# Neighbourhood queries and keys written with channels on partitions, and the recurrent branch woven in by its 48 steps

## The chip, the cores and the metric

One core of one Trainium2 chip runs the whole program. The metric is the device time in microseconds (us) of one execution, lower being better. Engines: PE (TensorE) multiplies, ACT (ScalarE), DVE (VectorE) and POOL (GpSimd) work elementwise, SP only issues DMAs; ACT issues DMAs too.

## The reference

Two layers of a block over 1280 tokens (256 of context, 1024 latent) of width 1024, in fp32. Each layer projects the modulated input `x` and feeds four branches: A, neighbourhood attention; B, latent attention; C, a gated linear recurrence; D, grouped-query attention. What matters here is the projection of A and the recurrence C:

```python
lat = split_cols(p_lat[..., :MIX_COLS], MIX_SPLITS)      # p_lat = modulated x @ w_in
q, k, v = (split_heads(tt, NA_HEADS) for tt in lat[0:3]) # branch A: 256 + 256 + 256 columns
...
x_c = centred_depthwise_conv(x, conv_w, conv_b)          # branch C
r = sigmoid(x_c @ w_a + b_a); i = sigmoid(x_c @ w_x + b_x)
log_a = -LRU_C * r * softplus(-lam)
a = exp(log_a); u = sqrt(-expm1(2.0 * log_a)) * (i * x_c)
h = linear_scan(a, u, h0, reverse)                       # one scan per direction, summed
```

The second layer has no use for queries of the context tokens.

## The kernel before, in words

**Precision.** Each fp32 operand is held as a high and a low half, and a product is three passes on PE: high by high, high by low, low by high. So a projection of 128 tokens over 1024 input channels is 8 chunks of 128 channels times 3 passes, 24 products. `x` lies in SBUF with channels on partitions, so that either operand can stand still: `mm_a` (L294, products at L299 to L301) holds 128 tokens of `x` in the array and streams weights, giving tokens on partitions; `mm_b` (L303, L307 to L309) holds 128 columns of weights and streams tokens, giving channels on partitions.

**Branch A's projection**, `a_steps` (L801), uses `mm_a`: per tile of 128 tokens it streams 512 columns (256 of queries, 256 of keys) into one PSUM bank; the second layer's two context tiles stream the 256 columns of keys alone. ACT copies the queries' half, scaled by 1/8 (L808), and the keys' half (L809) to SBUF. One tile later `put_t` (L340) turns it: four PE transposes (L348) into another bank, an ACT cast to the high half (L312), a DVE subtraction for the low half (L313), and two DMAs on ACT's queue (L355) to `qk_a` in DRAM, in runs of 128 tokens. Ten more tiles of 256 columns give the values (`put_v`, L358: cast, subtraction, one DMA at L362). `project` (L388) does eight tiles one by one and the last two chunk by chunk together.

**Branch C**, `lru_steps` (L470), goes twice over 128 channels (c = 0, 1). Each time: 24 products per token group into the three-bank tile `wide` (`sbank`), ACT copies (L481), DVE's convolution (L484, L489), a cast and a subtraction (L312, L313), then for each direction six sets of three gate products into `wide` with sigmoids on ACT (L515), and the chain tanh (L522) and exp (L523) on ACT, L526, L527 and L521 on DVE, square root on ACT (L528), L529 and two scans (L531, L532 or L535, L537) on DVE. ACT loads a table of functions (ACT_TABLE_LOAD) when it changes between sigmoid or tanh, exp, and square root. Then the directions are added (L541), and the branch's SiLU gate z is projected by `put_u` (L440; L459, L460, L466), and the result stored (L468).

**What sets the order.** `weave` (L83) runs streams of steps, always the one with the smallest (done + 0.5) / n; n is a number that the caller gives. Here (L950) the main stream, `m_proj`, one step of loads for the first attention, then `a_proj`, has n = W_A = 30, and the recurrence n = W_B = 26. The main stream has 33 steps in each layer (12 + 1 + 20); the recurrence has 48 in the first and 40 in the second. A scheduler behind that orders each engine's instructions by their dependences, so the printed orders below are not the programmed order to the step. The attention loop starts when both streams have ended; `cut_memory` (L953) closes the pool of large tiles and opens a new one over the same memory, so the first score tile of attention (written by L641) takes memory that the recurrence has used. `g_att__mm` are products of the merge gates, which fill PE between the score products (L639), transposes (L584) and value products (L591, L592) of attention.

**Buffers.** `mm` is a ring of two PSUM banks, shared by the projections, z and the gates; the high halves `ph` have three SBUF buffers, the low halves `pl` two.

Of the kernel before, what the change touches and what calls it, by code (L numbers as in the profile page):

```python
# [8 lines left out]
F32 = mybir.dt.float32  # L9
F32R = mybir.dt.float32r  # L10
AF = mybir.ActivationFunctionType
ALU = mybir.AluOpType
# [5 lines left out]
KC = D // 128  # L18
# [15 lines left out]
G_LAG = 1  # L34
X_ACT = (0, 2)
M_ORDER = (2, 3, 1, 0)
W_A = 30
W_B = 26
Z_0, GATE_0 = 2, 10
UNITS = [(2, 3), (5, 3), (8, 2)]  # L40
AHEAD = 2
# [6 lines left out]
def hybrid_kernel(ctx: ExitStack, tc, a):  # L48
    nc = tc.nc
    pe, act, dve, pool, sp = nc.tensor, nc.scalar, nc.vector, nc.gpsimd, nc.sync  # L50
# [3 lines left out]
    tp = ctx.enter_context(tc.tile_pool(name="tp", bufs=2))  # L54
# [21 lines left out]
    def nm(s):  # L76
        ids[0] += 1
        return f"{phase[0]}__{s}_{ids[0]}"
# [32 lines left out]
    def mm():  # L111
        return ps_mm.tile([128, 512], F32, tag="mm", name=nm("mm"))
# [9 lines left out]
    def tbank():  # L122
        turns[2] = (turns[2] + 1) % 3
        if wide_t[0] and not turns[2]:
            return ps_v.tile([128, 512], F32, tag="pv", name=nm("t"))
        return ps_t.tile([128, 512], F32, tag="t", name=nm("t"))
# [20 lines left out]
    def tmp(w=512, dt=F32):  # L147
        return tp.tile([128, w], dt, tag="tmp", name=nm("tmp"), bufs=3)
# [154 lines left out]
    def mm_b(ps, ws, xs, first=True, last=True):  # L303
        nk = len(ws)
        for k in range(nk):
            (wh, wl), (xh, xl) = ws[k], xs(k)
            pe.matmul(ps, wh, xh, start=first and k == 0, stop=False)  # L307
            pe.matmul(ps, wh, xl, start=False, stop=False)  # L308
            pe.matmul(ps, wl, xh, start=False, stop=last and k == nk - 1)  # L309

    def hi_lo(hi, lo, src):
        act.copy(hi, src)  # L312
        dve.tensor_sub(lo, src, hi)  # L313

    def layer(l, xh, xl, need_ctx, gate, finish, side, ahead=None):
        w_in = a["w_in"][l]
        q0t = 0 if need_ctx else CT
        groups = [(0, 256), (256, 512), (768, 512)]
        qgroups = groups if need_ctx else groups[1:]
# [7 lines left out]
        def xs_g(g):  # L327
            gs = slice(g[0], g[0] + g[1])
            return lambda k: (xh[:, k, gs], xl[:, k, gs])

        def dram(shape, dt, s):
            return dr.tile(shape, dt, tag=s, name=nm(s))

        qk_a = dram([2, 4, 128, NT], F32, "qka")
# [8 lines left out]
        def put_t(dst, t, first, src):  # L343

            n = len(src)
            pt = tbank()
            for i, s in enumerate(src):
                pe.transpose(pt[:, i * 128:(i + 1) * 128], s, ident)  # L348
            hi = tp.tile([128, 4, 128], F32R, tag="ph", name=nm("th"), bufs=3)
            lo = tp.tile([128, 4, 128], F32R, tag="pl", name=nm("tl"), bufs=2)  # L350
            p3 = pt.rearrange("p (a b) -> p a b", a=4)
            hi_lo(hi[:, :n, :], lo[:, :n, :], p3[:, :n, :])
            ts = slice(t * 128, (t + 1) * 128)
            for d, s in enumerate((hi, lo)):
                act.dma_start(dst[d, first:first + n, :, ts].rearrange("c p t -> p c t"), s.bitcast(F32)[:, :n, :])  # L355
# [20 lines left out]
        def project(ws, first_col, n, take=mm):  # L376

            for t in range(TT - 2):
                ps = take()
                c0 = first_col(t)  # L380
                mm_a(ps[:, c0:n], xs_t(t), ws, c0, n)
                yield t, ps
            c0 = first_col(TT - 2)
            last = [(t, mm()) for t in range(TT - 2, TT)]
            for k in range(KC):
                for t, ps in last:
                    xs = xs_t(t)
                    mm_a(ps[:, c0:n], lambda j: xs(k), ws[k:k + 1], c0, n, k == 0, k == KC - 1)  # L388
            yield from last
# [410 lines left out]

        def a_steps():  # L801
            wa = load_rows(w_in, C_A, 512)
            prev = None
            for t, ps in project(wa, lambda t: 0 if t >= q0t else 256, 512):
                c0 = 0 if t >= q0t else 256
                y = tmp()
                if c0 == 0:
                    act.activation(y[:, :256], ps[:, :256], AF.Copy, scale=0.125)  # L808
                act.copy(y[:, 256:], ps[:, 256:])  # L809
                if prev:  # L810
                    put_t(*prev)
                prev = qk_a, t, c0 // 128, [y[:, c:c + 128] for c in range(c0, 512, 128)]
                yield
            put_t(*prev)
            wv = load_rows(w_in, C_AV, 256)
            for t, ps in project(wv, lambda t: 0, 256):
                put_v(v_a, t, ps[:, :256].rearrange("p (h e) -> p h e", e=64))
                yield
# [126 lines left out]
        def first_loads():  # L945
            next(att)
            yield


        weave(("", chain((f"m_proj{l}", m_steps()), (f"g_att{l}", first_loads()), (f"a_proj{l}", a_steps())), W_A),  # L950
              (f"lru{l}", lru_steps(), W_B))
        wide_t[0] = False
# [93 lines left out]
        for batch in batches:  # L1046
            pairs = [(t, slot(w=D, s="Y")) for t in batch]
            for h in range(2):
# [5 lines left out]
                for t, Y in pairs:  # L1054
                    if chunks:
                        split_sum(chunks.pop(0))
                    s = 1 if t < CT else 0
# [3 lines left out]
                    ps = bank()  # L1061
# [205 lines left out]
```

## Time and profile before

| | us |
|---|---|
| median of three runs (2957.03 to 2962.0) | 2960.34 |
| the profiled execution's own time | 2960.92 |
| its span in the trace | 2959.1 |
| PE busy in the span | 2790.4 (94%) |
| DVE, ACT, POOL busy | 1508.0, 1219.0, 418.8 |

Times in the trace are counted from the start of the span; 1.8 us of the execution lie outside it. In the trace the first layer's `a_proj` runs on PE from 217 to 374 us and its recurrence from 125 to 404 us, and attention begins at 399 us; in the second layer `a_proj` runs from 1821 to 1968 us, the recurrence from 1726 to 1984 us, and attention begins at 1985 us. Rows of a stretch give busy time of each engine, and PEclk, the granted clock of TensorE as a share of its full speed. The bracket behind an instruction is the idle time of its engine before it and what ended that. A matmul's duration includes the time to drain; what the stream pays is the distance from one start to the next.

### The profile page before, as it was taken

The page shows a single profiled execution, that of the slowest core. Times are in us where ns is not written, and L with a number is a line of the kernel's source. Part 1 is how long each engine was busy: PE and PEld are TensorE (multiplying, and loading weights), DVE is VectorE, ACT ScalarE, POOL GpSimd, SP SyncE. Part 2 cuts the span into 40 slices and gives each one's busy share as a digit, 9 for nine tenths or more (in the row PEclk, how much of TensorE's full clock was granted, in tenths as well). Part 3 has the DMA queues.
Part 4 walks back from the last instruction along what each step waited for, and adds up shares of the span by engine and source line. Part 5 has one row for each costly group of instructions (what it writes and reads, how often), then busy time and mean ns, then how long its engine had stood idle before and what let it go on. Part 6 is the DMA issues. An engine that isn't in the chain of part 4 may idle for free.

```text
span 2959.1 us, 40218 instructions
## 1 busy us (share of the span) xinstructions
PE 2790.4 (94%) x14458; PEld 2253.0 (76%) x14458; DVE 1508.0 (51%) x3069; ACT 1219.0 (41%) x2631; POOL 418.8 (14%) x507
## 2 busy tenths in 40 slices
PE   7997979999999999899999798999999999999998
PEld 3785858888888887677767576778888888777776
DVE  5644266555555552232458554356555556533456
ACT  4344256445455542222234434346545455522230
POOL 1210020110111100111222120012111111001131
PEclk9998989999999999999999898999999999999999
DMA  6333322222223333333332333423222323222232
GB/s 248 115 107 102 107 72 84 84 84 87 88 88 123 103 98 111 104 120 104 124 98 90 91 103 111 117 74 102 80 93 78 106 103 126 87 94 87 86 109 91
DMA packets 240424, 301.83 MB, mean 102 GB/s; under 512 B 27488, under 2 KB 160096, under 8 KB 240224
## 3 DMA queue, kind: packets, MB, share of 16 engines
q1 hardware_dynamic: 134368, 225.58, 24.2%
q10 hardware_dynamic: 105856, 73.68, 8.0%
q8 instruction: 114, 1.87, 0.3%
q14 instruction: 86, 0.70, 0.1%
HBM read 217.11 MB, written 82.07 MB: 101 GB/s over the span
## 4 chain that ended last, share of the span: by engine, by line
PE 75%; DVE 7%; DMA 4%; ACT 4%; issue 2%; POOL 2%; ACTq 1%; SPq 0%; DVEq 0%; POOLq 0%
PE wide L639 6%; PE merge__mm L307 4%; PE merge__mm L308 4%; PE merge__mm L309 4%; PE wide L307 3%; PE wide L308 3%; PE wide L309 3%; PE m_att__t L584 3%; PE g_att__t L584 2%; PE a_att__mm L307 2%; PE a_att__mm L308 2%; PE a_att__mm L309 2%; PE m_att__mm L309 2%; PE m_att__mm L308 2%; PE m_att__mm L307 2%
## 5 line engine op out<-in xcount | busy, mean ns | idle before, releaser
L307 PE MATMUL merge__mm<-xh,merge__whi 128*128 128x512 f32 (+1 forms) x640 | 243.0, 380 | 0.9 <-ACT a_att__tmp L934 0.9
L308 PE MATMUL merge__mm<-xl,merge__whi 128*128 128x512 f32 (+1 forms) x640 | 239.6, 374 | 0.0
L309 PE MATMUL merge__mm<-xh,merge__wlo 128*128 128x512 f32 (+1 forms) x640 | 239.4, 374 | 0.0
L313 DVE TENSOR_TENSOR m_att__pl<-m_att__t,m_att__ph 128x384 fp32r<-128x384 f32 (+1 forms) x248 | 122.1, 508 | 117.2 <-ACT m_att__ph L312 78.8
L263 ACT CAST merge__whi<-merge__wraw 128x256 fp32r<-128x256 f32 (+1 forms) x128 | 65.6, 513 | 255.6 <-PE merge__mm L308 176.7
L1002 DVE TENSOR_TENSOR merge__tmp<-wide,merge__tmp 128x512 f32<-128x512 f32 (+1 forms) x120 | 76.5, 637 | 184.8 <-PE wide L309 161.2
L1003 POOL TENSOR_TENSOR merge__acc<-merge__acc,merge__tmp 128x512 f32<-128x512 f32 (+1 forms) x60 | 79.2, 1320 | 585.9 <-DVE merge__tmp L1002 585.8
L307 PEld LDWEIGHTS merge__mm<-xh,merge__whi 128*128 128x128 f32 x640 | 120.6, 188 | 44.5 <-issue 19.9
L312 ACT CAST m_att__ph<-m_att__t 128x384 fp32r<-128x384 f32 (+1 forms) x248 | 105.0, 439 | 115.3 <-PE m_att__t L584 103.5
L313 DVE TENSOR_TENSOR g_att__pl<-g_att__t,g_att__ph 128x384 fp32r<-128x384 f32 (+1 forms) x228 | 111.3, 514 | 79.6 <-ACT g_att__ph L312 58.4
L307 PE MATMUL wide<-merge__uh,merge__whi 128*128 128x256 f32 (+1 forms) x320 | 127.4, 398 | 20.4 <-ACT merge__uh L312 11.5
L264 DVE TENSOR_TENSOR merge__wlo<-merge__wraw,merge__whi 128x256 fp32r<-128x256 f32 (+1 forms) x128 | 71.0, 555 | 141.2 <-ACT merge__whi L263 134.3
L309 PEld LDWEIGHTS merge__mm<-xh,merge__wlo 128*128 128x128 f32 x640 | 120.8, 189 | 23.9 <-issue 0.4
L308 PEld LDWEIGHTS merge__mm<-xl,merge__whi 128*128 128x128 f32 x640 | 120.8, 189 | 22.3
L312 ACT CAST g_att__ph<-g_att__t 128x384 fp32r<-128x384 f32 (+1 forms) x228 | 97.7, 446 | 69.3 <-PE g_att__t L584 65.3
L307 PE MATMUL a_att__mm<-xh,a_att__whi 128*128 128x512 f32 (+1 forms) x320 | 123.8, 387 | 0.0
L641 DVE TENSOR_SCALAR_CACHE_REDUCE m_att__p<-wide 128x1280 f32<-128x1280 f32 (+1 forms) x72 | 98.7, 1371 | 42.1 <-PE wide L639 41.8
L309 PE MATMUL a_att__mm<-xh,a_att__wlo 128*128 128x512 f32 (+1 forms) x320 | 120.1, 377 | 0.0
L639 PE MATMUL wide<-g_att__ks,g_att__q 128*128 128x512 f32 (+1 forms) x400 | 103.5, 365 | 17.5 <-DVE g_att__p L641 16.3
L308 PE MATMUL a_att__mm<-xl,a_att__whi 128*128 128x512 f32 (+1 forms) x320 | 120.0, 375 | 0.0
L299 PE MATMUL a_proj__mm<-a_proj__whi,xh 128*128 128x256 f32 (+1 forms) x320 | 112.0, 351 | 8.1 <-ACT a_proj__tmp L809 4.5
L308 PE MATMUL wide<-merge__ul,merge__whi 128*128 128x256 f32 (+1 forms) x320 | 119.6, 374 | 0.0
(418 smaller groups left out, 7919.4 us busy)
## 6 DMA issues: line engine op xcount, KB each, us to landing
merge__wraw<-in_w_chunks_dram SPq DMA_DIRECT2D x64, 256.0 KB, 2.9
mod__wm<-in_w_mod_dram SPq DMA_DIRECT2D x64, 256.0 KB, 3.0
g_proj__wm<-in_w_mod_dram SPq DMA_DIRECT2D x16, 512.0 KB, 9.8
a_att__wraw<-in_w_chunks_dram SPq DMA_DIRECT2D x32, 256.0 KB, 2.7
merge__wraw<-in_w_branch_dram SPq DMA_DIRECT2D x64, 128.0 KB, 2.1
merge__tmp<-start__gates SPq DMA_DIRECT2D x32, 256.0 KB, 3.2
merge__tmp<-outp__gates SPq DMA_DIRECT2D x32, 256.0 KB, 3.4
g_att__wraw<-in_w_chunks_dram SPq DMA_DIRECT2D x28, 256.0 KB, 2.7
```

Source lines behind the costliest of these rows:

```text
L264: (pool if by_pool else dve).tensor_sub(lo[:, :n], raw[:, :n], hi[:, :n])
L299: pe.matmul(ps, xh, wh[:, n0:n1], start=first and k == 0, stop=False)
L307: pe.matmul(ps, wh, xh, start=first and k == 0, stop=False)
L308: pe.matmul(ps, wh, xl, start=False, stop=False)
L309: pe.matmul(ps, wl, xh, start=False, stop=last and k == nk - 1)
L312: act.copy(hi, src)
L313: dve.tensor_sub(lo, src, hi)
L584: pe.transpose(tb[:, i * 128:(i + 1) * 128], pts[q0 + i][:, col:col + 128], ident)
L639: pe.matmul(wide[:, c0:c0 + w], qs[:, j, qi * 128:(qi + 1) * 128], k[:, c0:c0 + w], start=j == 0, stop=j == len(ks) - 1)
L641: dve.tensor_scalar(pt[:, :nk], wide[:, :nk], -scale, None, ALU.mult, ALU.min, accum_out=nb)
L1002: dve.tensor_mul(sgm[:, :g[1]], pb[:, :g[1]], sgm[:, :g[1]])
L1003: (pool if w is None else dve).tensor_add(acc[c][:, gs], acc[c][:, gs], sgm[:, :g[1]])
```

## The change

Queries and keys are projected by `mm_b`: for each of the four blocks of 128 columns and each token group (256, 512 and 512 tokens; the second layer's queries leave out the first) the weights stand still and the tokens stream. The bank then holds channels on partitions already, so the transposes and the tile between are gone: one ACT operation writes the high half, scaled for queries (L814), one DVE operation the low half (L815), and two DMAs on ACT's queue store them (L817) in runs of 256 or 512 tokens. Twelve such items take the place of ten tiles in the first layer, ten items in the second. The values' part is as it was. W_A becomes 32 and W_B 48. The main stream then has 35 steps in the first layer and 33 in the second.

```diff
-W_A = 30
-W_B = 26
+W_A = 32
+W_B = 48
...
         def a_steps():
             wa = load_rows(w_in, C_A, 512)
-            prev = None
-            for t, ps in project(wa, lambda t: 0 if t >= q0t else 256, 512):
-                c0 = 0 if t >= q0t else 256
-                y = tmp()
-                if c0 == 0:
-                    act.activation(y[:, :256], ps[:, :256], AF.Copy, scale=0.125)
-                act.copy(y[:, 256:], ps[:, 256:])
-                if prev:
-                    put_t(*prev)
-                prev = qk_a, t, c0 // 128, [y[:, c:c + 128] for c in range(c0, 512, 128)]
+            items = [(c, g) for c in range(4) for g in (qgroups if c < 2 else groups)]
+
+            def part(c, g, ps, ks):
+                xs = xs_g(g)
+                ws = [(wh[:, c * 128:(c + 1) * 128], wl[:, c * 128:(c + 1) * 128]) for wh, wl in wa]
+                mm_b(ps[:, :g[1]], [ws[k] for k in ks], lambda j: xs(ks[j]), ks[0] == 0, ks[-1] == KC - 1)
+
+            def keep(c, g, ps):
+                n, scale = g[1], 0.125 if c < 2 else 1.0
+                hi = tp.tile([128, 512], F32R, tag="ph", name=nm("th"), bufs=3)
+                lo = tp.tile([128, 512], F32R, tag="pl", name=nm("tl"), bufs=2)
+                act.activation(hi[:, :n], ps[:, :n], AF.Copy, scale=scale)
+                dve.scalar_tensor_tensor(lo[:, :n], ps[:, :n], scale, hi[:, :n], ALU.mult, ALU.subtract)
+                for d, s in enumerate((hi, lo)):
+                    act.dma_start(qk_a[d, c, :, g[0]:g[0] + n], s.bitcast(F32)[:, :n])
+
+            for c, g in items[:-2]:
+                ps = mm()
+                part(c, g, ps, list(range(KC)))
+                keep(c, g, ps)
                 yield
-            put_t(*prev)
+
+            last = [(c, g, mm()) for c, g in items[-2:]]
+            for k in range(KC):
+                for c, g, ps in last:
+                    part(c, g, ps, [k])
+            for c, g, ps in last:
+                keep(c, g, ps)
+                yield
             wv = load_rows(w_in, C_AV, 256)
             for t, ps in project(wv, lambda t: 0, 256):
                 put_v(v_a, t, ps[:, :256].rearrange("p (h e) -> p h e", e=64))
```

**Where the instructions stand: the end of the first layer's projections, PE.** The four `wide` products with `lru__` operands are gate products of the second channel block (c = 1), `g_att__mm` products of the merge gates, and L639 attention's scores. Before, from the last gate products on:

```order
L309 MATMUL wide<-lru__lruh_3281,lru__gl_3296 128x256
L307 MATMUL g_att__mm_3524<-xh,g_att__whi_3514 128x256
L308 MATMUL g_att__mm_3524<-xl,g_att__whi_3514 128x256
L307 MATMUL g_att__mm_3652<-xh,g_att__whi_3514 128x512
L307 MATMUL wide<-lru__lruh_3281,lru__gh_3295 128x512
L308 MATMUL wide<-lru__lrul_3282,lru__gh_3295 128x512
L309 MATMUL wide<-lru__lruh_3281,lru__gl_3296 128x512
```

With the change, the last products ahead of attention's scores at the same place:

```order
L301 MATMUL a_proj__mm_3398<-a_proj__whi_3093,xl 128x256
L299 MATMUL a_proj__mm_3399<-a_proj__whi_3093,xh 128x256
L300 MATMUL a_proj__mm_3399<-a_proj__wlo_3094,xh 128x256
L301 MATMUL a_proj__mm_3399<-a_proj__whi_3093,xl 128x256
L639 MATMUL wide<-g_att__ks_2376,g_att__q_2380 128x256 x2
L584 MATMUL g_att__t_3514<-ident,g_att__p_3469 128x128
```

The gate products of c = 1 no longer stand there; the last pair of value tiles (`a_proj__mm_3398` and `3399`) does.

**The same place, DVE.** L526 to L541 and L466 are the recurrence's last chain, L641 is attention's first evacuation of scores. Before:

```order
L526 TENSOR_TENSOR lru__lruo_3366<-lru__lrug_3336 128x1280
L527 SCALAR_TENSOR_TENSOR lru__lrut_3362<-lru__lruo_3366,lru__lrut_3362 128x1280
L521 TENSOR_TENSOR lru__lrug_3349<-lru__lrug_3349,lru__lruc_3273 128x1280
L529 TENSOR_TENSOR lru__lrug_3349<-lru__lrug_3349,lru__lrut_3362 128x1280
L535 SCALAR_TENSOR_TENSOR lru__lruo_3366<-lru__lrug_3336,lru__lrug_3349 128x256
L537 SCALAR_TENSOR_TENSOR lru__lruo_3366<-lru__lrug_3336,lru__lruo_3366,lru__lrug_3349 128x1024
L541 TENSOR_TENSOR lru__lruo_3329<-lru__lruo_3329,lru__lruo_3366 128x1280
L466 SCALAR_TENSOR_TENSOR lru__lruo_3329<-lru__lruo_3329,lru__tmp_3411 128x256
L466 SCALAR_TENSOR_TENSOR lru__lruo_3329<-lru__lruo_3329,lru__tmp_3440 128x512
L466 SCALAR_TENSOR_TENSOR lru__lruo_3329<-lru__lruo_3329,lru__tmp_3469 128x512
L641 TENSOR_SCALAR g_att__p_3487,g_att__nb_3488<-wide 128x256
```

With the change:

```order
L466 SCALAR_TENSOR_TENSOR lru__lruo_2849<-lru__lruo_2849,lru__tmp_3335 128x512
L313 TENSOR_TENSOR a_proj__vt_3364<-a_proj__mm_3339,a_proj__vt_3364 128x4x64
L313 TENSOR_TENSOR a_proj__vt_3394<-a_proj__mm_3369,a_proj__vt_3394 128x4x64
L641 TENSOR_SCALAR g_att__p_3469,g_att__nb_3470<-wide 128x256
L313 TENSOR_TENSOR a_proj__vt_3448<-a_proj__mm_3398,a_proj__vt_3448 128x4x64
L313 TENSOR_TENSOR a_proj__vt_3452<-a_proj__mm_3399,a_proj__vt_3452 128x4x64
L641 TENSOR_SCALAR g_att__p_3475,g_att__nb_3476<-wide 128x256
```

The scans and sums have gone from in front of L641; four evacuations of value tiles stand around it.

**Where the chain has gone: DVE in the query and key part, with the change.** L815 frees the PSUM bank of an item (`a_proj__mm`), L526 to L532 are the first direction's chain of c = 1:

```order
L815 SCALAR_TENSOR_TENSOR a_proj__tl_2840<-a_proj__mm_2814,a_proj__th_2839 128x512
L526 TENSOR_TENSOR lru__lruo_2849<-lru__lrug_2788 128x1280
L527 SCALAR_TENSOR_TENSOR lru__lrut_2845<-lru__lruo_2849,lru__lrut_2845 128x1280
L521 TENSOR_TENSOR lru__lrug_2801<-lru__lrug_2801,lru__lruc_2704 128x1280
L529 TENSOR_TENSOR lru__lrug_2801<-lru__lrug_2801,lru__lrut_2845 128x1280
L815 SCALAR_TENSOR_TENSOR a_proj__tl_2882<-a_proj__mm_2856,a_proj__th_2881 128x512
L531 SCALAR_TENSOR_TENSOR lru__lruo_2849<-lru__lrug_2788,lru__lrug_2801 128x256
L532 SCALAR_TENSOR_TENSOR lru__lruo_2849<-lru__lrug_2788,lru__lruo_2849,lru__lrug_2801 128x1024
L815 SCALAR_TENSOR_TENSOR a_proj__tl_2939<-a_proj__mm_2913,a_proj__th_2938 128x256
```

The release of item 2856 stands behind four operations of the recurrence, and that of the next item, 2913, behind two scans; before, this chain of c = 1 stood behind all evacuations of `a_proj`.

## Rows read from the trace of the kernel before

**Rows 1.** The page: busy time by engine, and the chain that ended last.

```profile
PE 2790.4 (94%) x14458; PEld 2253.0 (76%) x14458; DVE 1508.0 (51%) x3069; ACT 1219.0 (41%) x2631; POOL 418.8 (14%) x507
...
PE 75%; DVE 7%; DMA 4%; ACT 4%; issue 2%; POOL 2%; ACTq 1%; SPq 0%; DVEq 0%; POOLq 0%
```

**Rows 2.** Busy time by stretch, from 200 to 430 us and in the second layer.

```profile
core 0: us, PE busy (x) PEld busy (x) DVE busy (x) ACT busy (x) POOL busy (x), PEclk, DMA share, GB/s
374.00:388.00 14.00, 12.31 (x65) 9.90 (x65) 3.94 (x6) 9.78 (x13) 0.00 (x0) 1.00 0.13 37
388.00:430.00 42.00, 25.13 (x108) 19.33 (x106) 27.94 (x23) 21.76 (x27) 18.11 (x12) 0.80 0.28 91
200.00:272.00 72.00, 52.91 (x219) 40.82 (x218) 35.23 (x71) 38.32 (x78) 4.86 (x9) 0.81 0.43 125
...
300.00:374.00 74.00, 73.91 (x458) 65.16 (x456) 20.48 (x36) 16.99 (x40) 0.52 (x1) 1.00 0.35 102
1863.00:1985.00 122.00, 116.64 (x640) 97.91 (x638) 45.99 (x60) 49.50 (x82) 0.53 (x1) 1.00 0.30 86
```

**Rows 3.** PE's instructions in time, 400 to 425 us.

```profile
400.35 0.63 PE L307 MATMUL wide<-lru__lruh,lru__gh 128*128 128x512 f32 x1
400.77 0.63 PE L308 MATMUL wide<-lru__lrul,lru__gh 128*128 128x512 f32 x1
...
424.95 0.80 PE L639 MATMUL wide<-g_att__ks,g_att__q 128*128 128x256 f32 x2 [14.01 <-DVE g_att__p L641]
```

**Rows 4.** DVE's instructions in time, 405 to 425 us.

```profile
405.27 1.65 DVE L526 TENSOR_TENSOR lru__lruo<-lru__lrug 128x1280 f32<-128x1280 f32 x1 [5.83 <-ACT lru__lrug L523]
...
411.34 1.71 DVE L529 TENSOR_TENSOR lru__lrug<-lru__lrug,lru__lrut 128x1280 f32<-128x1280 f32 x1
...
414.76 2.51 DVE L537 TENSOR_TENSOR_SCAN lru__lruo<-lru__lrug,lru__lruo,lru__lrug 128x1024 f32<-128x1024 f32 x1
...
424.47 0.42 DVE L641 TENSOR_SCALAR_CACHE_REDUCE g_att__p<-wide 128x256 f32<-128x256 f32 x1 [3.13 <-DMA start__u<-lru__lruo]
```

**Rows 5.** PE's instructions in time, 296 to 297 us: the transposes.

```profile
296.21 0.39 PE L301 MATMUL a_proj__mm<-a_proj__whi,xl 128*128 128x512 f32 x1
296.44 0.60 PE L348 MATMUL a_proj__t<-ident,a_proj__tmp 128*128 128x128 f32 x4
296.79 0.47 PE L307 MATMUL lru__mm<-xh,lru__whi 128*128 128x512 f32 x1
```

**Rows 6.** PE's products of line 348, both layers (ns: least, median, most).

```profile
L348 PE MATMUL a_proj__t<-ident,a_proj__tmp x76: 270/273/473, 259.8 to 1917.3; 128*128 128x128 f32 x76
```

**Rows 7.** Groups by line, 272 to 374 us: busy time, mean ns of one.

```profile
L313 DVE TENSOR_TENSOR a_proj__tl<-a_proj__t,a_proj__th 128x512 fp32r<-128x512 f32 x9 | 6.1, 691 | 31.1 <-ACT a_proj__th L312 29.0 <-DMA start__qka<-a_proj__tl 2.1
...
L312 ACT CAST a_proj__th<-a_proj__t 128x512 fp32r<-128x512 f32 x9 | 5.3, 606 | 1.9 <-PE a_proj__t L348 1.9
...
L489 DVE SCALAR_TENSOR_TENSOR lru__lruc<-lru__lrux,lrucols,lru__lruc 128x255 f32<-128x255 f32 (+3 forms) x5 | 3.7, 801 | 0.0
...
L808 ACT ACTIVATE a_proj__tmp<-a_proj__mm 128x256 f32<-128x256 f32 x8 | 3.1, 383 | 30.7 <-PE a_proj__mm L301 30.7
```

**Rows 8.** PE's instructions in time, 357 to 358 us: products of 256 columns.

```profile
357.10 0.28 PE L299 MATMUL a_proj__mm<-a_proj__whi,xh 128*128 128x256 f32 x1
357.22 0.28 PE L300 MATMUL a_proj__mm<-a_proj__wlo,xh 128*128 128x256 f32 x1
```

**Rows 9.** Weight loads (PEld) in time, the same stretch.

```profile
357.34 0.19 PEld L299 LDWEIGHTS a_proj__mm<-a_proj__whi,xh 128*128 128x128 f32 x1
```

**Rows 10.** ACT's instructions in time, 402 to 404 us: a load of a table of functions.

```profile
402.57 1.28 ACT L523 ACT_TABLE_LOAD   x1
```

## The prediction

> **What bounds the kernel now.** I first read the page's totals: PE is busy for 94% of the span and the chain that ended last lies on PE for 75%, on DVE for 7% [rows 1]. So PE sets the pace, and time is to be had where PE idles, where its clock is low, or by giving it less to do. Next I cut the region of the change into stretches [rows 2]. Three differ. From 300 to 374 us, where branch A's tiles run beside a quiet recurrence, PE is busy for 73.91 of 74 us at full clock: a PE instruction taken away there shortens the program by its own spacing. From 200 to 272 us, where the recurrence's first channel block (c = 0) does its gates and scans under the end of `m_proj` and the start of `a_proj`, PE is busy for 52.91 of 72 us and the clock is 0.81: 19.1 us idle. From 374 to 430 us is the tail: the projections are over, the second block (c = 1) still has its gates and scans to do, and PE idles 1.69 + 16.87 = 18.6 us at a clock of 0.80 from 388 us on. In the second layer, by contrast, the stretch around c = 1 (1863 to 1985 us) has 5.4 us idle at full clock.
>
> What holds the tail is seen on PE and DVE. PE's longest wait is 14.01 us before the score products at 424.95 us, for L641 on DVE [rows 3]. DVE at that time works through the recurrence's last chain, L526 at 405.27 us to L537, which ends at 417.27 us, then the sums, and L641 waits 3.13 us more until the recurrence's output is stored, since its tile takes that memory [rows 4]. That is a cause of order: the 33 main steps end when the recurrence, at 26/30 of a step each, has done 28.6 of its 48.
>
> **The change part by part.** The sum is made against the profiled execution, 2960.92 us (span 2959.1 and 1.8 outside); the median of the runs is 0.6 us less.
>
> *Products.* The first layer's query and key products go from 240 of 512 columns to 96 of 256 and 192 of 512. A product of 512 columns starts 0.23 us after the one before [rows 5], one of 256 columns 0.12 us [rows 8]: 240 x 0.233 = 55.9 us against 96 x 0.117 + 192 x 0.233 = 56.0. The second layer has the same 240 before and after. Cost nothing. The 48 added weight loads take 0.19 us each [rows 9], longer than a product of 256 columns, and yet these follow each other at 0.12 us, so loads go on beside products: nothing again. By the Trainium skill's page "TensorE: Matmul & The Clock Gate", section "The mechanism" (of packing), a weight load overlaps with products in flight only when it goes to other row groups, and all these fill all rows; that speaks against the change, and is a rival below. These rows do not agree with it.
>
> *Transposes.* 76 go (40 and 36) [rows 6]. Four take from 296.44 to 296.79 us [rows 5], 0.35 us, so 76 x 0.0875 = **6.6 us**, in a place where PE has no slack [rows 2]. It could not be more than 76 x 0.273 = 20.7 us, their recorded durations [rows 6], which overlap; nor under nothing.
>
> *Evacuation.* Per tile two ACT copies of 0.38 us [rows 7], a cast of 0.61 and a subtraction of 0.69 go; per item one ACT and one DVE operation on the same 512 columns come, which I take at those same 0.61 and 0.69 us. ACT loses work (0.38 + 0.38 + 0.61 us per tile become 0.61 per item), DVE keeps its own, ACT's queue issues 4 DMAs more in the first layer and none in the second, with longer runs; SP and POOL keep theirs. The low half still has two buffers; for their stores DVE waited 2.1 us in all from 272 to 374 us [rows 7]. None of this is on the path while the next item covers it: an item is 24 products, 5.6 us (2.8 for the 256-column group), against 1.3 us of evacuation. But something changes here that can cost: before, a bank of `mm` was freed by two ACT copies; now it is free only after DVE's L815, so it stands in DVE's queue behind whatever the recurrence has there. ACT also loads its tables twice more in all, 1.28 us each [rows 10], beside the path.
>
> *The recurrence's place.* At 48/32 = 1.5 steps per main step its 48 steps are done at main step 32 of 35, its 40 of the second layer after 27 of 33. So the first layer's tail goes: **18.6 us** of idle, and the clock that went with it. A mean clock of 0.80 over 42 us is 16.8 us at the lower of the two levels, 1.2 of 2.4 GHz [rows 2]; at 400 us products of 512 columns indeed start 0.42 us apart [rows 3]. Of these 16.8 us between 2.8 and 16.8 are work, since 14.0 us of the stretch are the one long wait; work at half speed loses half its time, so 1.4 to 8.4 us, and I take **4 us**, nearer the lower end because that wait comes in the middle of it.
>
> What is late next is the query and key part. There c = 1's convolution, gates and scans now stand among the twelve items. I walked the printed order with these durations: 1.3 us of evacuation; seven operations of the convolution at 0.8 us [rows 7], 5.6 us; the DVE chain L526 to L529, 405.27 to 413.05 us, 7.8 us; the scans behind it, to 417.27 us, 4.2 us [rows 4]. PE then stalls five times: 1.0 us for the cast behind the convolution, 2.0 us when item 2955 wants the bank of 2856, whose L815 waits behind the chain, 0.3 us for that of 2913, behind the scans, 3.0 us when z wants the bank of 2955, and 3.1 us in all for the values' weights, whose casts stand behind the gate functions on ACT. Together **9.4 us**, with bounds of nothing (the next item covers all) and 19.1 us, what c = 0's same work leaves idle under `m_proj` [rows 2]. I take the walk. Clock lost by it: up to 10 us if it falls as from 200 to 272 us (0.19 of 52.91), nothing if as from 1863 to 1985 us, where 5.4 us of spread stalls left it at 1.00 [rows 2]; stalls this spread are nearer the second, but longer, and I take 4 us.
>
> c = 0 moves earlier into `m_proj` by the same pace; I take its 19.1 us as unchanged, give or take 8. In the second layer c = 1's work moves from the values' part into the queries and keys: its stalls there, by the same walk about 8 us, take the place of the 5.4 us now and some behind them: nothing, give or take 6.
>
> Sum: -18.6 - 4 + 9.4 + 4 - 6.6 = **-15.8 us**, 2960.9 - 15.8 = 2945.1 us, forecast **2945**. The unknowns (8, 6, the walk's 9.4 both ways) reach from about -30 to -2 when two of them fall together.
>
> **The rivals.** A measurement here can tell about 0.2%, 5.9 us.
>
> *The stalls don't show.* If DVE's chains fall into the cover of the items (DVE is busy for only 20.48 of 74 us and ACT for 16.99 from 300 to 374 us [rows 2]), the 9.4 + 4 us are not paid, and the second layer saves some 3: -32, 2929 us. Against it: the ring has two banks, and the chain is 7.8 us where an item covers 5.6 or 2.8.
>
> *The wait only moves.* The stalls come to the upper bound, 19.1 us, with a clock loss of some 4 to 10: the tail's 22.6 is eaten, and the transposes alone remain, less a microsecond or so: about -3, 2958 us. For it: c = 0 is this very work in such a place. Against it: there much of the idle time is `m_proj`'s own chain of norms.
>
> *Slower: the bank waits for DVE.* In both layers each of c = 1's bursts now holds L815, thus a bank, thus PE. The burst less the cover of one item: the two chains with their scans and L815, 7.8 + 4.2 + 0.7 = 12.7 us each, less 5.6, are 7.1; twice per layer and in two layers 28 us; the convolution 5.6 less a 256-column item 2.8, 6 us in both; at a loss of clock as from 200 to 272 us, half a microsecond per microsecond idle, that is 34 x 1.5 = 51 us, against 22.6 + 6.6 and the second layer's 5.4 x 1.5 = 8: +14, **2975 us**. It decides from the point where the stalls of both layers' query and key parts exceed (22.6 + 6.6 + 8) / 1.5 = 25 us. Against it: the printed order puts L815 between the chain and the scans, not behind both, and the two directions' chains partly overlap with the ring's slack.
>
> *Weight loads aren't hidden.* Then 48 x 0.19 = 9.1 us [rows 9] come back, all in the first layer: -6.7, 2954 us. That is the rule of the page named above, taken at this trace's duration. Rows 8 and 9 speak against it.
>
> **How the numbers follow.** The forecast, give or take 10 us: 0.45. Stalls that don't show: 0.20. The wait only moves: 0.18. Slower: 0.14. Loads not hidden: 0.03, two thirds of it still faster. The first two are faster by over 5.9 us, the third and the rest of the last within it, the fourth above: faster 0.67, same 0.19, slower 0.14. The range takes in the second case with some microseconds more and the third whole, and leaves out about half of the slower case and the far end of the second: 2922 to 2968 us.
>
> **What would show it.** Right: from the last value tiles on PE goes straight to the scores, with no wait over 2 us for L641, and the scores that now follow at 424.95 us follow at about 412 (18.6 + 4 - 13.4 + 40 x 0.0875 = 12.7 us sooner). The query and key part shows PE waits of 0.3 to 3 us that name L815 and L814. Products of 256 columns stand 0.12 us apart in L307 to L309 too. Wrong: PE idle of over 19 us between the first item and the last value tile of the first layer (the wait only moved), or over 25 us in both layers (slower); a granted clock under 0.9 throughout the query and key part; a wait for L641 that remains, because its tile waits for some other store.

## The result, and the profile after

| | before | change |
|---|---|---|
| median, us | 2958.69 (2955.18 to 2962.0, 4 runs) | 2927.11 (2920.24 to 2932.83, 4 runs) |
| ratio | | 0.9892 [0.9867, 0.9918] |
| profiled execution, us | 2960.92 | 2928.52 |

The change is faster by 31.6 us (24 to 39), twice the 15.8 that were forecast; the time lies in the range, 18 us under the forecast and beside that of the first rival (2929). A second measurement gave 0.9887 [0.9869, 0.9906].

The page's totals move little (compare [rows 1]): PE is busy for 16 us less, and the shares of the chain are the same.

```profile
PE 2774.3 (95%) x14430; PEld 2242.8 (77%) x14430; DVE 1499.7 (51%) x3071; ACT 1214.4 (41%) x2597; POOL 417.5 (14%) x507
...
PE 75%; DVE 7%; DMA 4%; ACT 4%; issue 2%; POOL 2%; ACTq 0%; SPq 0%; POOLq 0%; DVEq 0%
```

The stretches that answer to [rows 2], cut where the work now falls: `m_proj`'s end and the first items (200 to 295 us), the other items and the values (295 to 402), the start of attention, and in the second layer most of the items and the values (columns as in [rows 2]):

```profile
200.00:295.00 95.00, 75.89 (x352) 61.27 (x353) 46.05 (x98) 40.41 (x87) 6.56 (x12) 0.89 0.48 143
295.00:402.00 107.00, 100.35 (x584) 86.05 (x582) 42.28 (x54) 41.85 (x61) 0.00 (x0) 1.00 0.24 80
402.00:430.00 28.00, 26.10 (x150) 21.66 (x151) 16.30 (x32) 16.58 (x33) 11.36 (x12) 1.00 0.46 141
...
1860.00:1958.00 98.00, 92.69 (x532) 79.28 (x531) 43.05 (x55) 41.79 (x60) 0.00 (x0) 0.98 0.26 85
```

The tail is gone. Where PE idled for 18.6 of the 56 us from 374 on, at a clock of 0.80 from 388 us, it now idles for 6.7 of 107 us at full clock. DVE is busy for 42.28 us there, where it had 20.48 in the 74 us from 300 on: the recurrence's chains have moved under the items. PE at the joint with attention answers to [rows 3]:

```profile
401.43 0.27 PE L301 MATMUL a_proj__mm<-a_proj__whi,xl 128*128 128x256 f32 x1
402.23 0.50 PE L639 MATMUL wide<-g_att__ks,g_att__q 128*128 128x256 f32 x2 [0.53 <-DVE g_att__p L641]
```

The wait of 14.01 us for L641 is 0.53. These scores stand at 402.2 us in place of 424.95; attention as a whole gains less, 16.2 us at its last score product, since before PE had done some `g_att__mm` products while it waited, and they come later now.

What PE waits for in the changed stretch (PE waits from 270 to 402 us; total us, times, longest us):

```profile
PE a_proj__mm L307 <- DVE a_proj__tl L815: 4.4, 2, 3.6
PE lru__mm L307 <- DVE a_proj__tl L815: 2.5, 1, 2.5
PE a_proj__mm L299 <- ACT a_proj__whi L263: 1.2, 1, 1.2
PE a_proj__mm L300 <- DVE a_proj__wlo L264: 1.0, 1, 1.0
PE wide L307 <- ACT lru__lrug L515: 0.8, 1, 0.8
```

These are 9.9 us in sum, but only 6.3 of them are stalls of the kind that the prediction walked through (9.4 us): 2.5 and 0.8 us for a bank that L815 has not freed behind c = 1's chains, 1.2 and 1.0 for the values' weights, 0.8 for a gate. The longest, 3.6 us, is another. It stands at the joint with `m_proj`, 30 us ahead of c = 1's convolution on DVE: L815 of the first item is held up behind subtractions of `m_proj`, which wait for their stores (DVE, then PE in time):

```profile
278.57 0.56 DVE L313 TENSOR_TENSOR m_proj__tl<-m_proj__t,m_proj__th 128x384 fp32r<-128x384 f32 x1 [5.54 <-DMA start__qkm<-m_proj__tl]
281.39 0.43 DVE L815 SCALAR_TENSOR_TENSOR a_proj__tl<-a_proj__mm,a_proj__th 128x256 fp32r<-128x256 f32 x1 [1.00 <-DMA start__qkm<-m_proj__tl]
...
281.87 0.49 PE L307 MATMUL a_proj__mm<-xh,a_proj__whi 128*128 128x512 f32 x1 [3.64 <-DVE a_proj__tl L815]
283.65 0.63 PE L307 MATMUL a_proj__mm<-xh,a_proj__whi 128*128 128x512 f32 x1
284.07 0.63 PE L308 MATMUL a_proj__mm<-xl,a_proj__whi 128*128 128x512 f32 x1
```

The last two rows show the clock behind that stall: products of 512 columns start 0.42 us apart for 3 us, the lower of the two levels. The first rival's number came out, and of its mechanism one half: the clock is hardly lost, but the stalls are there.

### The profile page after: what moved, and what is told of

It is laid out like the page before. It is cut to its first block, busy times and chain, and to the rows that moved or that the text cites. A ratio compares the mean times of both kernels' runs of the same rounds, so it can differ in the third digit from the quotient of the medians.

```text
span 2926.5 us, 40088 instructions
## 1 busy us (share of the span) xinstructions
PE 2774.3 (95%) x14430; PEld 2242.8 (77%) x14430; DVE 1499.7 (51%) x3071; ACT 1214.4 (41%) x2597; POOL 417.5 (14%) x507
## 4 chain that ended last, share of the span: by engine, by line
PE 75%; DVE 7%; DMA 4%; ACT 4%; issue 2%; POOL 2%; ACTq 0%; SPq 0%; POOLq 0%; DVEq 0%
PE wide L639 6%; PE merge__mm L307 4%; PE merge__mm L308 4%; PE merge__mm L309 4%; PE wide L307 3%; PE wide L308 3%; PE wide L309 3%; PE m_att__t L584 3%; PE g_att__t L584 2%; PE a_att__mm L307 2%; PE a_att__mm L308 2%; PE m_att__mm L308 2%; PE m_att__mm L309 2%; PE a_att__mm L309 2%; PE m_att__mm L307 2%
## 5 line engine op out<-in xcount | busy, mean ns | idle before, releaser
L641 DVE TENSOR_SCALAR_CACHE_REDUCE g_att__p<-wide 128x1280 f32<-128x1280 f32 (+1 forms) x72 | 98.6, 1369 | 47.0 <-PE wide L639 36.7
L641 DVE TENSOR_SCALAR_CACHE_REDUCE m_att__p<-wide 128x1280 f32<-128x1280 f32 (+1 forms) x72 | 98.7, 1371 | 41.9 <-PE wide L639 41.6
L309 PE MATMUL wide<-merge__uh,merge__wlo 128*128 128x256 f32 (+1 forms) x320 | 118.4, 370 | 0.0
```

The lines of the kernel that those rows point to most:

```text
L641: dve.tensor_scalar(pt[:, :nk], wide[:, :nk], -scale, None, ALU.mult, ALU.min, accum_out=nb)
```

## The experiments

All were timed against the kernel before on the same chip; us saved are the ratio applied to some 2961 us.

| run | ratio | us saved |
|---|---|---|
| change_again | 0.9887 [0.9869, 0.9906] | 33 (28 to 39) |
| e1_weave_alone | 0.9950 [0.9937, 0.9963] | 15 (11 to 19) |
| e2_projection_alone | 0.9949 [0.9936, 0.9962] | 15 (11 to 19) |
| e3_first_layer | 0.9910 [0.9895, 0.9925] | 27 (22 to 31) |
| e4_second_layer | 0.9943 [0.9931, 0.9955] | 17 (13 to 20) |
| e5_no_transposes | 0.9964 [0.9950, 0.9978] | 11 (7 to 15) |
| e9_weave_no_transposes | 0.9943 [0.9929, 0.9957] | 17 (13 to 21) |
| e10_transposes_twice | 1.0001 [0.9992, 1.0010] | 0 (-3 to 2) |
| e6_other_banks | 0.9905 [0.9891, 0.9919] | 28 (24 to 32) |
| e7_pace_64 | 0.9888 [0.9873, 0.9904] | 33 (28 to 38) |
| e8_low_in_tmp | 0.9909 [0.9896, 0.9923] | 27 (23 to 31) |
| e11_pace_64_other_banks | 0.9854 [0.9833, 0.9875] | 43 (37 to 49) |

**The two parts apart.** In the kernel before:

```diff
-W_A = 30
-W_B = 26
+W_A = 32
+W_B = 48
```

> The old projection with its transposes, with W_A = 32 and W_B = 48. Theory A (the time came from the recurrence's place, in both layers, and the transposes are a small sum of their own: 75 gaps of about 0.115 us between their starts, 8.6 us): the 31.6 us of the whole change less 8.6, so about 23 us under before, 2936 us. Rival B (the two parts need each other: with two copies, a cast and turned banks per tile the old evacuation collides with the recurrence once they run together): under 13 us gained, 2946 us or more. Rival C (the projection brought most of it): within 6 us of before.

And the changed kernel with the two numbers put back:

```diff
-W_A = 32
-W_B = 48
+W_A = 30
+W_B = 26
```

> The new projection with the old W_A = 30 and W_B = 26. Theory A: only the transposes go, 8.6 us under before, about 2950 us, and the long wait for L641 at the end of the first layer's projections stays at over 10 us. Rival B: the same, 2950 us. Rival C: 20 us or more under before, 2939 us or less.

Each brings 15 us, and together they bring 33: about the sum, though not layer by layer, as will be seen. None of the three theories has both numbers. Theory A gave the weave too much and the projection, at its transposes' 8.6 us, too little; B comes near the weave's 15 (it said under 13) but not the projection's; C is wrong on the weave. The trace of the second shows the long wait halved without any new numbers, but not the tail gone (PE waits from 374 to 430 us, the two longest groups):

```profile
PE wide L639 <- DVE g_att__p L641: 6.5, 2, 6.0
PE g_att__mm L307 <- POOL g_att__whi L261: 3.7, 1, 3.7
```

The long wait is 6.0 us where it was 14.01, but others have come ahead of it: PE still idles for 15.6 of these 56 us, where it idled for 18.6. The new projection has twelve items where there were ten tiles, so the main stream of the first layer has 35 steps, and at 26/30 a step the recurrence has done 30.3 of its steps by the end of it, not 28.6. That would account for the shorter wait; it was not tried by itself.

**By layer.** The changed kernel with the new numbers in the first layer alone, and, with `l == 1` in the same places, in the second alone:

```diff
-        weave(("", chain((f"m_proj{l}", m_steps()), (f"g_att{l}", first_loads()), (f"a_proj{l}", a_steps())), W_A),
-              (f"lru{l}", lru_steps(), W_B))
+        weave(("", chain((f"m_proj{l}", m_steps()), (f"g_att{l}", first_loads()), (f"a_proj{l}", a_steps())), W_A if l == 0 else 30),
+              (f"lru{l}", lru_steps(), W_B if l == 0 else 26))
```

> The new projection in both layers, the new weave numbers in the first layer alone, the second at 30 and 26. The two traces give 16.2 us to the first layer and 16.4 to the second. Theory A: the second layer keeps its transposes alone (4.1 us) and gives back about 12 us: 16 + 4 = 20 us under before, 2939 us. Rival D (the prediction on record: the second layer's recurrence gains nothing by its new place, and what the traces show there has another cause): within 4 us of the whole change, 2927 to 2931 us.

> The mirror of the run before: the new weave numbers in the second layer alone. Theory A: 16 us of the second layer and 4.5 us of the first layer's transposes, 20 us under before, 2938 us, with the 14 us wait for L641 in the first layer back. Rival D: the transposes alone, 8.6 us, about 2950 us.

Over the projection alone (2945.72 us in the same series) the first layer's new place brings 9.4 us (2936.36) and the second's 2.7 (2943.05). Of both together (17 to 18 us beyond the projection's 15) some 5 us stay unassigned, within what two such ratios can tell. Counted the other way, from the run with the second layer's new place (17) to the whole change (33), the first layer's brings 16. Theory A's 20 us for each is not met: the first has more, the second less. Theory D is not met to the letter either, but for the second layer it is nearer: 3 to 6 us there, not 12.

The traces can be split by layer too. The first layer is counted from the start of the span to the last score product of its neighbourhood attention, the second from the last transpose of the first layer's output (L238) to the last score product of its own. These are the score products (L639) of the first layer, before, with the projection alone and with the change; the numbers behind the durations are the first and the last start:

```profile
L639 PE MATMUL wide<-g_att__ks,g_att__q x208: 275/392/794, 407.7 to 620.7; 128*128 128x512 f32 x64, 128*128 128x256 f32 x40
L639 PE MATMUL wide<-g_att__ks,g_att__q x208: 274/392/795, 407.5 to 620.3; 128*128 128x512 f32 x64, 128*128 128x256 f32 x40
L639 PE MATMUL wide<-g_att__ks,g_att__q x208: 276/392/505, 353.6 to 604.5; 128*128 128x512 f32 x64, 128*128 128x256 f32 x40
```

| what runs in the layer (us; one number per trace) | first layer | second layer |
|---|---|---|
| before | 620.7 | 522.6 |
| before, transposes twice (e10) | 622.2 | 518.0 |
| before, no transposes (e5) | 617.7 | 508.9 |
| new weave numbers alone (e1) | 615.3 | 512.4 |
| new weave numbers, no transposes (e9) | 612.6 | 507.8 |
| projection alone (e2; e4's first layer, e3's second) | 620.3, 617.0 | 508.4, 510.4 |
| both (change, change_again; e3's first layer, e4's second) | 604.5, 601.5, 603.9 | 506.2, 504.2, 505.1 |
| both, pace 64 and other banks (e11, below) | 596.2 | 508.5 |

Between the two counted stretches runs code that no edit touches, and it takes 1023.0 to 1030.9 us; so a difference of a few us in one trace says nothing. Even so, the layers differ clearly. In the first, the parts need each other, as rival B had it: the projection alone brings 0 to 4 us, the weave alone 5, both 16 to 19. In the second they overlap: 12 to 14, 10, and 16 to 18 (each 5 less against e10, which has no less work than before). So by these traces it is chance that 15 and 15 make about 33.

**The transposes.** In the kernel before, `put_n` in place of `put_t`, which is the same without the transposes (`p3` is the copied tile):

```diff
-                    put_t(*prev)
-                prev = qk_a, t, c0 // 128, [y[:, c:c + 128] for c in range(c0, 512, 128)]
+                    put_n(*prev)
+                prev = qk_a, t, c0 // 128, y[:, c0:]
```

> The kernel before, with the four transposes of each of branch A's query and key tiles left out: the cast and the subtraction read the copied tile, which is stored untransposed. Everything else, the two ACT copies, the cast, the stores and the old weave numbers, stays. The projection alone brought 15 us where the prediction gave the transposes 6.6. Theory P (the prediction on record: a transpose costs PE its 0.0875 us and no more): 6 to 8 us under before. Theory Q (the transposes hold PE about 18 us: 0.35 us per group of four where their copies are early, 0.9 where they aren't, and 5.4 and 3.3 us at the two places where PE stands before them for ACT's copies): 11 to 18 us under before, most of what the projection brings. Theory R (the shorter evacuation on ACT brought the 15 us): within 6 us of before.

The same edit, with the two new numbers:

```diff
-W_A = 30
-W_B = 26
+W_A = 32
+W_B = 48
```

> The kernel before with the new weave numbers (32 and 48) and with the transposes of branch A's query and key tiles left out (stored untransposed), all else of the old projection kept. The weave alone brought 15 us, leaving out the transposes alone 11. Theory E (the two are separate times on PE and add up): 24 to 29 us under before. Theory F (both remove the same waits, once PE is late it covers them): 15 to 19 us. Theory G (the shorter evacuation of the new projection is what makes the new place worth while): under 26 us here, and over 6 us behind the change.

And the transposes kept and done twice (`times` is 2 in branch A's calls of `put_t`):

```diff
-            for i, s in enumerate(src):
+            for i, s in list(enumerate(src)) * times:
```

> The kernel before with each of the 76 transposes of branch A's query and key tiles done twice into the same place. This adds PE work and no wait for a copy. Theory P (PE's pure price is 0.0875 us each, and what else went with them is waiting for the copies on ACT): 5 to 9 us over before. Theory Q2 (each transpose costs PE more than its spacing, through weight loads and the change of operand): 12 to 20 us over before.

Left out, they bring 11 us (7 to 15), between theories P and Q; done twice they cost nothing (-2 to 3 us), which neither P nor Q2 allows. They were really done (the products of line 348, then busy time by stretch, of the run with them twice):

```profile
L348 PE MATMUL a_proj__t<-ident,a_proj__tmp x152: 270/272/477, 258.9 to 1918.0; 128*128 128x128 f32 x152
```

```profile
300.00:374.00 74.00, 74.00 (x466) 65.74 (x466) 19.13 (x35) 17.18 (x39) 0.53 (x1) 1.00 0.34 101
1863.00:1985.00 122.00, 118.96 (x673) 101.05 (x671) 45.46 (x59) 51.49 (x84) 0.52 (x1) 1.00 0.31 88
```

In the second layer the extra work went into time that PE idled before (busy 118.96 us in place of 116.64 [rows 2]). In the first, PE was full, and still is, and its end comes 1.5 us later, of the 3.5 us that 40 transposes are at 0.0875 us; the spacing may be paid in part there. The medians tell that of PE's 6.6 us at most 3 are on the path. Left out, the transposes bring the first layer 3.0 us, close to their spacing; the second layer becomes 13.7 us shorter, where the spacing of its 36 is 3.2. So most of the 11 us lies in the second layer, and it isn't PE's time for them. In that stretch PE idles for 41.6 us in place of 47.1, and the mean granted clock is 0.96 in place of 0.95, an estimated 5 us at most. Why is not shown: with the transposes twice the idle time is 41.6 us too. That leaving them out takes PE out of the way from a tile's copy to its cast, both on ACT, is an argument that no run here shows by itself. With the new weave numbers leaving them out brings next to nothing (17 against 15 us), which rules out theory E. F and G both fit: the weave already removes what the transposes cost (F), and what the new projection brings on top of the weave, 17 to 18 us, is not its transposes (G). The trace of e9 shows where it stands behind the change (PE waits from 340 to 372 us; line numbers are ten later there, so L525 is L515 and L649 is L639):

```profile
PE wide L307 <- ACT lru__lrug L525: 3.6, 5, 0.8
PE wide L649 <- ACT lru__lrug L525: 3.0, 1, 3.0
PE lru__mm L307 <- ACT lru__whi L263: 2.8, 1, 2.8
PE a_proj__mm L300 <- DVE a_proj__wlo L264: 1.8, 1, 1.8
PE a_proj__mm L299 <- ACT a_proj__whi L263: 1.1, 1, 1.1
```

12.3 us, where the change waits 6.3 from 320 to 370 us. And the clock is low there. Busy time by stretch, e9, then the change (columns as in [rows 2]):

```profile
340.00:372.00 32.00, 19.61 (x87) 14.99 (x86) 17.41 (x20) 17.93 (x26) 0.00 (x0) 0.68 0.33 98
340.00:372.00 32.00, 27.27 (x157) 22.97 (x156) 18.29 (x23) 17.30 (x26) 0.00 (x0) 1.00 0.33 109
```

PE idles for 12.4 us in e9 and 4.7 in the change, and what e9 does in that stretch it does for the most part at the lower level: a mean clock of 0.68 is 20 of the 32 us there. e1, with the transposes, is the same (17.54 us busy, 0.70); the change's second trace has 28.45 us and 0.95. This is where the old projection in the new place falls behind the change. The ten tiles are used up by 344 us, and the gate products of c = 1 then wait for one sigmoid after another with no products of the projection between them; in the change, whose items reach further, one such wait of 0.8 us is left.

**What is left: banks, pace, buffers.** The changed kernel with its items in the banks of the transposes:

```diff
-                ps = mm()
+                ps = tbank()
...
-            last = [(c, g, mm()) for c, g in items[-2:]]
+            last = [(c, g, tbank()) for c, g in items[-2:]]
```

> The changed kernel with its query and key items written to the three banks that the transposes used, in place of the ring of two which they share with z and the values. In the trace of the change PE waits for L815 to free a bank 3.6, 2.5 and 0.8 us in the first layer, 1.4 and 0.9 us in the second. Theory S (these waits lie on the path): they go, 5 to 9 us under the change, so 37 to 41 us under before. Theory T (the recurrence and the evacuations are the bound of that stretch and the wait turns up elsewhere): within 3 us of the change, 29 to 35 us under before.

With the recurrence woven in faster:

```diff
-W_B = 48
+W_B = 64
```

> The changed kernel with W_B = 64: the recurrence is woven at 2 steps per main step and has ended at main step 24 of 35. Theory A (what counts is that the recurrence ends before the projections do; pushed further it collides with the chain of norms in m_proj): no gain, 0 to 8 us slower than the change, 24 to 32 us under before. Theory U (the earlier the better, as the values' part then covers nothing that waits): 3 to 8 us under the change.

With the low halves in another ring:

```diff
-                lo = tp.tile([128, 512], F32R, tag="pl", name=nm("tl"), bufs=2)
+                lo = tp.tile([128, 512], F32R, tag="tmp", name=nm("tl"), bufs=3)
```

> The changed kernel with the low halves of the query and key items in the three buffers that the copied tiles used, no longer in the two which they share with m_proj. At the joint of m_proj and a_proj PE waits 3.6 us in the first layer and 6.3 us in the second, and DVE there waits up to 5.5 us for stores of m_proj's low halves. Theory V (L815 waits for one of those two buffers): the waits shrink, 3 to 6 us under the change. Theory W (L815 stands in DVE's queue behind m_proj's own subtraction, which waits for its store all the same): no change over 3 us.

And the first two together:

```diff
-W_B = 48
+W_B = 64
...
-                ps = mm()
+                ps = tbank()
```

> The changed kernel with W_B = 64 and its query and key items in the three banks of the transposes: two edits that each gave no measurable gain. Theory T (what is left there is bound by the recurrence's own chains and by the stores at the joint with m_proj): within 4 us of the change. Theory H (either edit moved its waits into what the other removes): 5 us or more under the change.

One by one nothing is gained: 28, 33 and 27 us against the change's 33, which is nearest to T, A and W as far as the intervals tell. Together the two are at 0.9854, 2917.66 us beside 2925.68 for the change on the same chip; the intervals touch (0.9875 and 0.9869), so 10 us (1 to 18) is the estimate from both. The trace of e11 is of the slowest of its five executions; its first layer ends at 596.2 us, 5 to 8 us sooner than in the change's two traces, and the rest of it gives that back. What PE waits for from 268 to 390 us, with other banks alone:

```profile
PE a_proj__mm L300 <- DVE a_proj__wlo L264: 4.0, 2, 3.3
PE wide L307 <- DVE m_proj__vt L313: 1.0, 1, 1.0
PE a_proj__mm L299 <- ACT a_proj__whi L263: 0.9, 1, 0.9
```

With pace 64 alone (its three longest):

```profile
PE wide L307 <- ACT lru__lrux L481: 4.9, 1, 4.9
PE wide L307 <- ACT lru__lrug L515: 2.7, 3, 1.5
PE lru__mm L307 <- DVE a_proj__tl L815: 2.5, 1, 2.5
```

With both:

```profile
PE wide L307 <- ACT lru__lrux L481: 0.9, 1, 0.9
PE wide L307 <- ACT lru__lrug L515: 0.8, 1, 0.8
```

With other banks no wait names L815, but PE is then early for the values' weights, whose casts stand behind c = 1's chain; with pace 64 that chain is over by then, but the banks are still waited for, and ACT's copies (L481) for longer. Each edit uncovers what the other removes, as theory H said. e8 rules out the buffers of the low halves as the cause of the wait at the joint with `m_proj`: with a ring of their own the program is no faster, and the longest wait there is 7.0 us, not 3.6 (the same view of e8, from 265 to 400 us):

```profile
PE a_proj__mm L307 <- DVE a_proj__tl L815: 7.7, 2, 7.0
```

## Why the prediction was right in sign and half in size

- **The tail** (-18.6 us of idle, -4 of clock): right. The 14.01 us for L641 went, and the clock is 1.00 from 295 to 430 us; what the clock gave back was not measured by itself. The scores came at 402.2 us, where the prediction had put them at about 412.
- **The stalls that take its place** (9.4 us by the walked order): right in kind, 6.3 us in size, with L815 as the release that is waited for longest. The 3.6 us at the joint with `m_proj` were not in the walk; that the sum of 9.9 comes so near 9.4 is chance. **The clock lost by them** (4 us): 1.00 from 295 us on, and behind the stall at the joint seven products of 512 columns at 0.43 us in place of 0.23, an estimated 1.4 us.
- So the **first layer's place**, forecast -9.2 us net, is measured at 9.4 (e3 against e2) or 16 (the change against e4), and the traces have 13 to 19. With 6.3 and 1.4 us in place of 9.4 and 4 the prediction's own sum gives -14.9. c = 0's share "unchanged": right, PE idles for 27.5 us from 100 to 300 us, where it idled for 26.7, at a clock of 0.93 both times.
- **The second layer's place** ("nothing, give or take 6"): 3 to 6 us gained, inside.
- **The transposes and the evacuation** (-6.6 us and nothing): this is the step that failed. The projection by itself brings 15 us (11 to 19). For the first layer, from whose rows the price was taken, the term is about right: 0 to 4 us by the traces for the projection alone, and 3.0 for the transposes alone, against 3.5. It fails in the second layer: 12 to 14 us (8 to 10 against e10) where 3.2 had been put, and leaving out the transposes gives as much without the new evacuation. It is not their spacing there, since PE is not full (116.64 of 122 us [rows 2]) and twice the transposes cost nothing. The prediction let a spacing in the first layer stand for all that a transpose holds up in the second. What that is stays open.
- **The parts as separate terms**: the sum adds the transposes' price to that of the new place, as if either came without the other. In the first layer they don't: on top of the weave the projection brings 11 to 14 us there (6 to 8 in the second layer), as the old projection waits for 12.4 us at a clock of 0.68 where the new one waits for 4.7 at 1.00 (e9). How much of that is due to items that reach further under the gates of c = 1 (35 main steps in place of 33), and how much to the single ACT operation that stands where two copies and a cast did, is open: no kernel was run that has the old projection in more, shorter steps. The steps are not the reason for the projection's 15 us by itself: the first layer, where they become 35, gains 0 to 4 us by it, and the second has 33 before and after.
- **Weight loads aren't hidden**: ruled out. Products of 256 columns with the weights standing start 0.12 us apart in the change too (PE in time):

```profile
315.77 0.28 PE L307 MATMUL a_proj__mm<-xh,a_proj__whi 128*128 128x256 f32 x1
315.88 0.28 PE L308 MATMUL a_proj__mm<-xl,a_proj__whi 128*128 128x256 f32 x1
```

  while a load takes 0.19 us [rows 9]. The rule of the Trainium skill's page "TensorE: Matmul & The Clock Gate", section "The mechanism", that a load overlaps only across row groups, does not hold for these rows; the same section also has a load into the background weight buffer go ahead of products, which they would fit.
- **Slower: the bank waits for DVE**: it does, for 3.3 us behind c = 1's bursts in the first layer and 3.6 behind `m_proj`'s subtractions, but not for each burst in full: DVE's queue has L815 between the chain's operations, and an item of 5.6 us covers most of one. The sign given for this case, over 25 us of idle in both layers' query, key and value parts, is just reached, 12.6 + 12.7 us in this trace (22.8 in the second), and the program is faster all the same; it was set too low.

## What to carry to other kernels

A price read from one stretch holds for that stretch: the same instruction can hold up more, or nothing, in another layer. Leaving it out and doubling it are two cheap tests of whether its own time is on the path, and the result has to be read stage by stage. Two parts of a change that seem to add up in the medians can need each other in one stage and overlap in another. Where two streams are interleaved by counts of steps, every edit that changes one stream's number of steps changes the pace of the other, and has to be costed as such. When a wait goes and nothing is gained, look for the one that it uncovered, and remove both.

## What the runs showed of the hardware

76 transposes added, 40 of them in the layer where PE is busy for 74 of 74 us, left the program's time as it was, 1.0001 [0.9992, 1.0010]; at most 3 of their 6.6 us of spacing can be in it. Products of 256 columns, each with a new weight load of 0.19 us, start 0.12 us apart. In 32 us in which PE idles for 12.4 the mean granted clock was 0.68 (e9), and in the same 32 us with 4.7 us of idle time 1.00 (the change). Single executions of one kernel differ by up to 17 us (2911.38 to 2928.38 for e11, whose profiled execution is the longest of them, and as long as the change's 2928.52), and 8 us of that kind of difference can lie in code that no edit touches. So a trace was read for which wait is there and for the layer that it falls in, and the medians for what it is worth.
